# A scaled and re-split input for the first feed-forward product, in 512- and 256-column matmuls

## The chip, the cores and the metric

The kernel runs on one core of a Trainium2 chip. The metric is the device time of one execution in microseconds (us). The engines are PE (matrix multiply, with PEld for its weight loads), DVE (vector), ACT (scalar, activations), POOL (GpSimd) and SP (which issues DMAs).

## What is computed

A decoder trunk of two layers over 256 tokens and 1024 features: layer 0 with differential attention, layer 1 with latent attention, and in both a feed-forward block with a causal convolution and a gated per-layer embedding. The change touches the feed-forward block alone:

```python
def rms_norm(x, gain):
    y = xf * lax.rsqrt(jnp.mean(xf * xf, axis=-1, keepdims=True) + RMS_EPS)
    return (y * gain.astype(jnp.float32)).astype(x.dtype)

def conv_gated_ffn(h, w_in, conv_w, conv_b, w_out):     # w_in: 1024 x 5632, w_out: 2816 x 1024
    u = h @ w_in
    u_pad = jnp.pad(u, ((0, 0), (CONV_WIDTH - 1, 0), (0, 0)))
    c = conv_b
    for j in range(CONV_WIDTH):                          # 3 taps
        c = c + u_pad[:, j:j + s, :] * conv_w[j]
    a, g = jnp.split(c, 2, axis=-1)
    return (jax.nn.silu(g) * a) @ w_out

h = h + conv_gated_ffn(rms_norm(h, ffn_norm[i]), ...)    # once a layer
```

## The kernel before

All activations lie with features on the 128 partitions and the 256 tokens along the free dimension; `hT[:, k]` is the k-th of 8 blocks of 128 features of the residual stream. Products are kept near float32 by splitting each operand into a high part (rounded to fp32r by a cast on ACT) and a low part, the remainder (a subtraction). Weights come from one array, `wall`, in units of 128 x 1024 floats that are loaded in the order of use (`fetch`, on SP's queue), cast on ACT into `wh` and subtracted on DVE or POOL into `wl` (`split_unit`). `share[0]` says which: it is added up unit by unit, and each time the sum passes 1 that unit's subtraction goes to POOL.

`mm3` makes one contraction step of three matmuls of 256 columns (high x high, high x low, low x high), with two different weights, `wh` and `wl`. `mm2` makes the same step of two: `wh` against high and low part of the input side by side (512 columns, the results in the two halves of a bank), and `wl` against the high part (256 columns). The two halves have to be added afterwards. The second feed-forward product (`wst` with `wide`) already uses `mm2`.

`ffn` works through 22 pairs, i = 0 to 21: a pair is 128 columns of the value half and the same 128 of the gate half, two weight units, each with 8 contraction steps. The input `hgH`, `hgL` is the residual times the norm's gain, split, without the factor 1/rms of each token: that factor is not known when the product starts. `rstd_diag` and `rstd_rows` compute it during pairs 0 to 2 and leave it as `rb`, a tile with 1/rms of the tokens along the columns, the same on all partitions. `evac(i, ps)` multiplies the finished pair in PSUM by `rb` (L800, one instruction for both halves, since both lie in one bank), then makes the convolution (ACT L805, DVE L806 and L807), silu (ACT L809), the product (DVE L810) and the split for the second product (`g[i]`). Pairs that end before `rb` is there wait in `todo`.

The order on the engines is made by a scheduler that works from its own estimates when the program is built, so instructions of neighbouring pairs mix. Each engine then runs its list strictly in order. PSUM has 8 banks, which all pairs go round (`bankW`).

Of the kernel before, what the change touches and what calls it, by code (L numbers as in the profile page):

```python
# [14 lines left out]
ALU = mybir.AluOpType  # L15
# [4 lines left out]
P = 128  # L20
S = 256
NT = 2
D = 1024
NK = D // P
# [15 lines left out]
C_FFN = (32, 40)  # L40
# [38 lines left out]
RATIO_B = 1.7  # L79
BANKS_B = "ABACBACAACAA"  # L80
SH_A = 0.5
SH_FFN = 0.4
SH_PLE = 0.5
SH_B = 0.3

# [9 lines left out]
def trunk(ctx, tc, xT, xN, pT, pos, consts, grow, wall, out):  # L95
    nc = tc.nc
    V, A, G, T = nc.vector, nc.scalar, nc.gpsimd, nc.tensor
# [9 lines left out]
    def bank(tag):  # L107
        return pools[tag].tile([P, 512], F32, tag=tag, name="p" + tag.lower())
# [7 lines left out]
    def bankT():  # L116
        return bank("T")
# [6 lines left out]
    def bankW():  # L124
        nwide[0] += 1
        return bank("ACACA"[nwide[0] % 5])

    def d_tile(n=512, dt=F32):
        if dt == F32R:
            return tmp.tile([P, 512], F32R, tag="dr", name="dr", bufs=BUF_DR)[:, :n]  # L130
        return tmp.tile([P, 512], F32, tag="d", name="d", bufs=BUF_D)[:, :n]
# [10 lines left out]
    def f(ap):  # L142
        return ap.bitcast(F32)
# [11 lines left out]
    def run(gen):  # L155
        for c in gen:
            assert c is not None or late
            pump(c is None)
# [37 lines left out]
    def mm3(ps, aH, aL, bH, bL, start, stop):  # L196
        clk[0] += 3 * max(0.107, bH.shape[-1] * 0.000427)
        T.matmul(ps, lhsT=aH, rhs=bH, start=start, stop=False)  # L198
        T.matmul(ps, lhsT=aH, rhs=bL, start=False, stop=False)  # L199
        lastmm[0] = T.matmul(ps, lhsT=aL, rhs=bH, start=False, stop=stop).ins  # L200

    def mm2(ps, aH, aL, b, start, stop):


        n = b.shape[-1]
        clk[0] += 3 * max(0.107, n * 0.000427)
        T.matmul(ps[:, :2 * n], lhsT=aH, rhs=b.rearrange("p c n -> p (c n)"), start=start, stop=False)  # L207
        lastmm[0] = T.matmul(ps[:, :n], lhsT=aL, rhs=b[:, 0], start=False, stop=stop).ins  # L208

    def split(hi, lo, src, scale=None):  # L210
        if scale is None:
            return A.copy(hi, src).ins, V.tensor_sub(lo, src, f(hi)).ins  # L212
        return (A.activation(hi, src, AF.Copy, scale=scale).ins,
                V.scalar_tensor_tensor(lo, src, scale, f(hi), ALU.mult, ALU.subtract).ins)  # L214


    hT = cp.tile([P, NK, S], F32, name="hT")
# [10 lines left out]
    def fetch(pieces=1):  # L228
        st = ring.tile([P, UNIT], F32, tag="st", name="st", bufs=BUF_ST)
        u, n = unit_no[0], UNIT // pieces  # L230
        unit_no[0] += 1
        for j in range(pieces):
            lastfetch[0] = nc.sync.dma_start(st[:, j * n:(j + 1) * n], wall[u, :, j * n:(j + 1) * n]).ins
            if u in hooks:
                hooks.pop(u)()
            if pieces > 1:
                yield st
        if pieces == 1:
            yield st
# [4 lines left out]
    def split_unit(st, pair=None):  # L244
        hi, lo = pair or ring_pair()
        turn[0] += share[0]
        eng = V
        if turn[0] >= 1.0:
            turn[0] -= 1.0
            eng = G  # L250
        A.copy(hi, st)  # L251
        eng.tensor_sub(lo, st, f(hi))  # L252
        return hi, lo

    def load_unit():
        return split_unit(next(fetch()))
# [11 lines left out]
    def col(c, n=1):  # L268
        return cst[:, c:c + n]
# [21 lines left out]
    def og():  # L291
        return act.tile([P, 4, S], F32R, tag="og", name="og", bufs=8)

    def qk():
        return act.tile([P, 2, S], F32R, tag="qk", name="qk", bufs=BUF_QK)
# [33 lines left out]
    def rstd_rows(dg):  # L329
        with tc.high_priority(), tc.issue_after(lastmm[0]):  # L330
            ps = bankT()
            T.matmul(ps[:, :S], lhsT=ones, rhs=dg, start=True, stop=True)
            rb = act.tile([P, S], F32, tag="rb", name="rb", bufs=1)
            A.copy(rb, ps[:, :S])
        return rb
# [311 lines left out]
    def wst(order, b, post, bank=bankA, wide=0):  # L647

        kn = 1 + max(k for _, k in order)
        pss = {}  # L650
        for i, (n, k) in enumerate(order):
            z = i % 8
            if z == 0:
                u = load_unit()
            if k == 0:
                pss[n] = bank()
            ps, c, p = pss[n], slice(z * P, (z + 1) * P), b(k)
            if n < wide:
                mm2(ps, u[0][:, c], u[1][:, c], p, k == 0, k == kn - 1)
            else:  # L660
                mm3(ps[:, :S], u[0][:, c], u[1][:, c], p[:, 0], p[:, 1], k == 0, k == kn - 1)
            if k == kn - 1:
                add_h(n, ps[:, :S], post, ps[:, S:] if n < wide else None)
                del pss[n]
            if z == 7:
                yield 1
# [60 lines left out]
    def pre_load(l):  # L727

        share[0], was = 1.0, share[0]
        w = {"p": ple_p(l), "w": [split_unit(next(fetch()), ring_pair("x", 2)) for _ in range(2)]}  # L730
        share[0] = was
        return w
# [42 lines left out]
    def two(hgH, hgL, sq):  # L775

        ps = [bankW()[:, :S] for _ in range(2)]
        us = [load_unit() for _ in range(2)]
        for k in range(NK):
            for p, u in zip(ps, us):  # L780
                mm3(p, u[0][:, k * P:(k + 1) * P], u[1][:, k * P:(k + 1) * P], hgH[:, k], hgL[:, k], k == 0,
                    k == NK - 1)
            if k == NK - 3:
                dg = rstd_diag(sq)
        return ps, dg

    def ffn(l, st, post, mid=None):
        hgH, hgL = st["hg"]
        g = {}
        rb = None  # L790
        todo = []

        def evac(i, ps):
            if isinstance(ps, list):
                us = ps
                for u in us:
                    V.tensor_mul(u, u, rb)
            else:
                w = ps.rearrange("p (s t) -> p s t", s=2)
                V.tensor_mul(w, w, rb.unsqueeze(1).to_broadcast([P, 2, S]))  # L800
                us = w[:, 0], w[:, 1]
            cc = d_tile().rearrange("p (s t) -> p s t", s=2)
            for s in range(2):
                c0 = C_CONV[l] + 4 * (s * NF + i)
                A.activation(cc[:, s], us[s], AF.Identity, bias=col(c0 + 3), scale=col(c0 + 2))  # L805
                V.scalar_tensor_tensor(cc[:, s, 1:], us[s][:, :S - 1], col(c0 + 1), cc[:, s, 1:], ALU.mult, ALU.add)  # L806
                V.scalar_tensor_tensor(cc[:, s, 2:], us[s][:, :S - 2], col(c0), cc[:, s, 2:], ALU.mult, ALU.add)  # L807
            pr = us[0]
            A.activation(us[1], cc[:, 1], AF.Silu)  # L809
            V.tensor_mul(pr, us[1], cc[:, 0])  # L810
            if i >= 16:
                g[i] = qk()
            elif i % 2 == 0:
                gt = og()
                g[i], g[i + 1] = gt[:, 0:2], gt[:, 2:4]
            split(g[i][:, 0], g[i][:, 1], pr)

        for i in range(NF):
            if i == 0:
                share[0] = 0.0  # L820
                ps, dg = two(hgH, hgL, st["sq"])
            else:
                ps = bankW()
                for s in range(2):
                    wH, wL = load_unit()
                    for k in range(NK):
                        mm3(ps[:, s * S:(s + 1) * S], wH[:, k * P:(k + 1) * P], wL[:, k * P:(k + 1) * P], hgH[:, k],
                            hgL[:, k], k == 0, k == NK - 1)
                    if i == 1 and s == 0:
                        rb = rstd_rows(dg)  # L830
            if i == 2:
                share[0] = SH_FFN
            todo.append((i, ps))
            if i == 8 and mid:
                mid()
            while rb is not None and todo:
                evac(*todo.pop(0))
        if l == 0:
            pj.append(pre_load(1))
        share[0] = 0.0  # L840
        run(wst(FFN_OUT_ORDER, lambda k: g[k], post, bankW, NK - 1))
# [106 lines left out]
    actx.close()  # L948
    share[0] = SH_FFN
    pq = {}  # L950
# [3 lines left out]

    st2 = {}
    ffn(0, st, prep_post(C_PLE[0], st2), mid0)

    kvs = {}
# [282 lines left out]
    bctx.close()  # L1241
    share[0] = SH_FFN
    st2 = {}
    ffn(1, st, prep_post(C_PLE[1], st2))

    def out_post(n):
# [138 lines left out]
```

## Time and profile before

| | us |
|---|---|
| median of 3 runs | 770.49 (769.53 to 770.62) |
| the execution that was profiled | 770.32 |
| its span | 768.5 |
| PE busy in the span | 748.9 |
| DVE busy | 578.1 |
| ACT busy | 484.1 |
| POOL busy | 252.4 |

Busy times are of one profiled execution. Matmuls are pipelined: one of 256 columns is listed with 0.28 us though the next starts 0.12 us after it. So the rate of PE, and of DVE and ACT too, is read from start to start. In the timelines an idle stretch in front of an instruction stands in brackets with what ended it. The first product of layer 0 runs from about 155 to 278 us, that of layer 1 from about 550 to 675.

### The profile page before, as it was taken

How to read it: one execution, taken by the hardware profiler on the slowest of the kernel's cores; microseconds unless marked ns; L12 is line 12 of the kernel's file. 1: busy time of each engine (PE TensorE's matmuls, PEld its weight loads, DVE VectorE, ACT ScalarE, POOL GpSimd, SP SyncE). 2: the span in 40 equal slices, each digit the busy share in tenths (PEclk: the TensorE clock that was granted, in tenths of full speed). 3: DMA queues.
4: the chain of work that ended last, by engine and by line, in shares of the span. 5: the costliest groups of instructions: out<-in, count | busy, mean ns of one | idle time of the engine just before them, and what ended most of it. 6: DMA issues, size and time to landing. Idle time of an engine off the chain costs nothing.

```text
span 768.5 us, 15843 instructions
## 1 busy us (share of the span) xinstructions
PE 748.9 (97%) x6088; PEld 720.2 (94%) x6088; DVE 578.1 (75%) x1160; ACT 484.1 (63%) x1043; POOL 252.4 (33%) x176
## 2 busy tenths in 40 slices
PE   8999999999999999999999999999999999999996
PEld 6998988999999998899889998999999999988896
DVE  6667898568997787647688998877588778876545
ACT  6537777676666665547867776654676666655442
POOL 2654454233333420211214563421342332201230
PEclk9999999999999999999999999999999999999999
DMA  8994444255665576655355133334456555555531
GB/s 297 261 225 186 120 153 153 85 170 182 195 190 184 161 271 194 202 179 165 122 177 169 57 104 100 120 118 139 137 195 192 171 185 194 189 186 178 188 108 56
DMA packets 37517, 127.94 MB, mean 166 GB/s; under 512 B 4672, under 2 KB 6208, under 8 KB 37440
## 3 DMA queue, kind: packets, MB, share of 16 engines
q1 hardware_dynamic: 36432, 126.29, 51.9%
q8 instruction: 48, 0.79, 0.4%
q10 hardware_dynamic: 1008, 0.63, 0.3%
q14 instruction: 29, 0.24, 0.1%
HBM read 125.75 MB, written 1.15 MB: 165 GB/s over the span
## 4 chain that ended last, share of the span: by engine, by line
PE 80%; DVE 6%; ACT 6%; DMA 4%; POOL 2%; issue 2%; SPq 0%; ACTq 0%; DVEq 0%; POOLq 0%
PE pa L198 14%; PE pa L200 13%; PE pa L199 13%; PE pc L200 6%; PE pc L199 6%; PE pc L198 6%; PE pa L207 6%; PE pc L207 3%; PE pa L208 3%; DMA oh<-s 3%; PE pc L208 2%; ACT wh L251 2%; DVE wl L252 2%; POOL wl L252 1%; DMA st<-in_wall 1%
## 5 line engine op out<-in xcount | busy, mean ns | idle before, releaser
L251 ACT CAST wh<-st 128x1024 fp32r<-128x1024 f32 x221 | 230.8, 1049 | 153.0 <-issue 57.4
L252 DVE TENSOR_TENSOR wl<-st,wh 128x1024 fp32r<-128x1024 f32 x166 | 210.5, 1270 | 89.7 <-ACT wh L251 77.1
L252 POOL TENSOR_TENSOR wl<-st,wh 128x1024 fp32r<-128x1024 f32 x55 | 134.8, 2450 | 206.4 <-ACT wh L251 198.0
L200 PE MATMUL pa<-hgH,wl 128*128 128x256 f32 x496 | 141.2, 285 | 0.4 <-POOL wl L252 0.4
L199 PE MATMUL pa<-hgL,wh 128*128 128x256 f32 x496 | 140.3, 283 | 0.0
L198 PE MATMUL pa<-hgH,wh 128*128 128x256 f32 x496 | 140.1, 283 | 0.0
L309 POOL TENSOR_TENSOR ssq<-ssq,d 128x256 f32<-128x256 f32 x35 | 36.3, 1037 | 188.9 <-ACT d L308 174.1
L200 PE MATMUL pc<-hgH,wl 128*128 128x256 f32 x336 | 95.4, 284 | 0.9 <-DVE wl L252 0.9
L200 PEld LDWEIGHTS pa<-hgH,wl 128*128 128x128 f32 x496 | 95.2, 192 | 0.7 <-POOL wl L252 0.6
L198 PE MATMUL pc<-hgH,wh 128*128 128x256 f32 x336 | 95.1, 284 | 0.4 <-DVE pa L810 0.4
L198 PEld LDWEIGHTS pa<-hgH,wh 128*128 128x128 f32 x496 | 95.1, 192 | 0.1
L199 PEld LDWEIGHTS pa<-hgL,wh 128*128 128x128 f32 x496 | 95.2, 192 | 0.0
L199 PE MATMUL pc<-hgL,wh 128*128 128x256 f32 x336 | 95.1, 283 | 0.1
L198 PE MATMUL pa<-wh,hgH 128*128 128x256 f32 x320 | 92.0, 291 | 1.5 <-ACT wh L685 0.8
L199 PE MATMUL pa<-wl,hgH 128*128 128x256 f32 x320 | 91.8, 288 | 1.5 <-DVE wl L252 0.8
L200 PE MATMUL pa<-wh,hgL 128*128 128x256 f32 x320 | 91.2, 286 | 0.7 <-DVE hgL L212 0.7
L200 PEld LDWEIGHTS pc<-hgH,wl 128*128 128x128 f32 x336 | 64.5, 192 | 1.4 <-DVE wl L252 1.4
L198 PEld LDWEIGHTS pc<-hgH,wh 128*128 128x128 f32 x336 | 64.4, 192 | 0.8 <-DVE pa L810 0.6
L199 PEld LDWEIGHTS pc<-hgL,wh 128*128 128x128 f32 x336 | 64.4, 192 | 0.3 <-DVE hgL L214 0.3
L199 PEld LDWEIGHTS pa<-wl,hgH 128*128 128x128 f32 x320 | 61.6, 192 | 3.0 <-DVE wl L252 1.2
L198 PEld LDWEIGHTS pa<-wh,hgH 128*128 128x128 f32 x320 | 61.1, 193 | 3.0 <-ACT wh L685 1.1
L200 PEld LDWEIGHTS pa<-wh,hgL 128*128 128x128 f32 x320 | 61.6, 192 | 1.1 <-DVE hgL L212 0.9
(319 smaller groups left out, 1888.7 us busy)
## 6 DMA issues: line engine op xcount, KB each, us to landing
st<-in_wall SPq DMA_DIRECT2D x225, 512.0 KB, 3.7
oh<-s SPq DMA_DIRECT2D x24, 128.0 KB, 7.4
hT<-in_x SPq DMA_DIRECT2D x4, 256.0 KB, 5.1
st<-in_wall SPq DMA_DIRECT2D x4, 256.0 KB, 5.3
st<-in_xn SPq DMA_DIRECT2D x2, 512.0 KB, 7.0
d<-in_p SPq DMA_DIRECT2D x2, 256.0 KB, 4.7
out_h<-hT SPq DMA_DIRECT2D x4, 128.0 KB, 2.0
out_h<-hT ACTq DMA_DIRECT2D x4, 128.0 KB, 2.0
```

The costliest lines, as they stand in the source:

```text
L198: T.matmul(ps, lhsT=aH, rhs=bH, start=start, stop=False)
L199: T.matmul(ps, lhsT=aH, rhs=bL, start=False, stop=False)
L200: lastmm[0] = T.matmul(ps, lhsT=aL, rhs=bH, start=False, stop=stop).ins
L207: T.matmul(ps[:, :2 * n], lhsT=aH, rhs=b.rearrange("p c n -> p (c n)"), start=start, stop=False)
L208: lastmm[0] = T.matmul(ps[:, :n], lhsT=aL, rhs=b[:, 0], start=False, stop=stop).ins
L251: A.copy(hi, st)
L252: eng.tensor_sub(lo, st, f(hi))
L309: sqlast[0] = G.tensor_add(sq, sq, t).ins
```

## The change

For i = 4 on (`SCALED`), the factor `rb` moves from the result to the input. `scaled` makes, once a layer, eight pairs of tiles: `hT[:, k]` times gain times `rb` (DVE, one instruction), then the split (ACT cast, DVE subtraction), with high and low part side by side in one `qk` tile. The pairs from the fifth on use `mm2` on these tiles, and gate and value have a bank each. Their `evac` has no multiplication by `rb`; it copies the right half of each bank to SBUF (ACT) and adds it to the left half (DVE). The share of POOL is set one pair later and is 0.5 in place of 0.4.

```diff
-SH_FFN = 0.4
+SH_FFN = 0.5
+SCALED = 4
...
+    def scaled(g, rb):
+        hs = []
+        for k in range(NK):
+            x, pair = d_tile(S), qk()
+            V.scalar_tensor_tensor(x, hT[:, k], col(g + k), rb, ALU.mult, ALU.mult)
+            split(pair[:, 0], pair[:, 1], x)
+            hs.append(pair)
+        return hs
...
         def evac(i, ps):
-            if isinstance(ps, list):
+            if i >= SCALED:
+                lo = d_tile().rearrange("p (s t) -> p s t", s=2)
+                us = [p[:, :S] for p in ps]
+                for s in range(2):
+                    A.copy(lo[:, s], ps[s][:, S:])
+                    V.tensor_add(us[s], us[s], lo[:, s])
+            elif isinstance(ps, list):
...
-            else:
+            elif i < SCALED:
                 ps = bankW()
...
+            else:
+                ps = [bankW() for _ in range(2)]
+                for s in range(2):
+                    wH, wL = load_unit()
+                    for k in range(NK):
+                        mm2(ps[s], wH[:, k * P:(k + 1) * P], wL[:, k * P:(k + 1) * P], hs[k], k == 0, k == NK - 1)
             if i == 2:
+                hs = scaled(C_FFN[l], rb)
+            elif i == 3:
                 share[0] = SH_FFN
```

DVE in layer 0, from the first use of `rb`, before. `pc_2456` and `pa_2457` are the two banks of the first pair, `pc_2528` that of the second, `pa_2619` of the third; `d_` tiles hold the convolution, `og_` the input of the second product, `wl_` a weight remainder:

```order
L797 TENSOR_TENSOR pc_2456<-pc_2456,rb_2561 128x256
L797 TENSOR_TENSOR pa_2457<-pa_2457,rb_2561 128x256
L800 TENSOR_TENSOR pc_2528<-pc_2528,rb_2561 128x512
L800 TENSOR_TENSOR pa_2619<-pa_2619,rb_2561 128x512
L806 SCALAR_TENSOR_TENSOR d_2595<-pc_2456,cst_83,d_2595 128x255
L806 SCALAR_TENSOR_TENSOR d_2595<-pa_2457,cst_83,d_2595 128x255
L807 SCALAR_TENSOR_TENSOR d_2595<-pc_2456,cst_83,d_2595 128x254
L252 TENSOR_TENSOR wl_2800<-st_2797,wh_2799 128x1024
L807 SCALAR_TENSOR_TENSOR d_2595<-pa_2457,cst_83,d_2595 128x254
```

The same place now. L793 writes the scaled input (`d_2680` to `d_2700` are its first five pieces, the five rows in a row), and L213 on `qk_` is the subtraction that finishes a piece:

```order
L814 TENSOR_TENSOR pc_2456<-pc_2456,rb_2561 128x256
L814 TENSOR_TENSOR pa_2457<-pa_2457,rb_2561 128x256
L817 TENSOR_TENSOR pc_2528<-pc_2528,rb_2561 128x512
L817 TENSOR_TENSOR pa_2619<-pa_2619,rb_2561 128x512
L823 SCALAR_TENSOR_TENSOR d_2595<-pc_2456,cst_83,d_2595 128x255
L793 SCALAR_TENSOR_TENSOR d_2680<-hT_82,cst_83,rb_2561 128x256
```

DVE some 22 instructions later, up to the row that finishes the last of the eight pieces (`qk_2716`), and the two behind it; `og_2604<-pc_2456` is the last to read the first bank of the first pair:

```order
L817 TENSOR_TENSOR pa_2733<-pa_2733,rb_2561 128x512
L793 SCALAR_TENSOR_TENSOR d_2710<-hT_82,cst_83,rb_2561 128x256
L827 TENSOR_TENSOR pc_2456<-pa_2457,d_2595 128x256
L823 SCALAR_TENSOR_TENSOR d_2721<-pa_2619,cst_83,d_2721 128x255
L213 TENSOR_TENSOR qk_2706<-d_2705,qk_2706 128x256
L823 SCALAR_TENSOR_TENSOR d_2795<-pa_2733,cst_83,d_2795 128x255
L213 TENSOR_TENSOR qk_2711<-d_2710,qk_2711 128x256
L213 TENSOR_TENSOR qk_2716<-d_2715,qk_2716 128x256
L824 SCALAR_TENSOR_TENSOR d_2721<-pa_2619,cst_83,d_2721 128x254
L213 TENSOR_TENSOR og_2604<-pc_2456,og_2604 128x256
```

Between the first use of `rb` and the row of `qk_2716` there stand now 32 instructions, both counted; before, the first evacuations went on at once.

PE where the fourth pair (`pa_2693`) ends and the next begins, before:

```order
L198 MATMUL pa_2693<-hgH_2343,wh_2726 128x256
L199 MATMUL pa_2693<-hgL_2344,wh_2726 128x256
L200 MATMUL pa_2693<-hgH_2343,wl_2727 128x256
L198 MATMUL pa_2840<-hgH_2343,wh_2843 128x256
L199 MATMUL pa_2840<-hgL_2344,wh_2843 128x256
```

And now; `pa_2733` is the fourth pair, `pa_2807` the gate's bank of the fifth:

```order
L199 MATMUL pa_2733<-hgH_2343,wh_2766 128x256
L200 MATMUL pa_2733<-hgL_2344,wh_2766 128x256
L201 MATMUL pa_2733<-hgH_2343,wl_2767 128x256
L208 MATMUL pa_2807<-qk_2681,wh_2832 128x512
L209 MATMUL pa_2807<-qk_2681,wl_2833 128x256
```

The fifth pair now reads the scaled tiles (`qk_`) from its first matmul on. Its other bank, `pc_2806`, comes after it and is the one that `pc_2456` had. On POOL, one weight remainder a pair now stands in the list from the fifth pair on; on ACT, eight casts of `qk_` tiles stand among the casts of `wh_`, in front of the table load for silu. SP's order is the same as before.

## Rows read from the trace of the kernel before

**Rows 1.** The page, part 4: shares of the chain that ended last

```profile
PE 80%; DVE 6%; ACT 6%; DMA 4%; POOL 2%; issue 2%; SPq 0%; ACTq 0%; DVEq 0%; POOLq 0%
```

**Rows 2.** By stretch: length; busy PE, PEld, DVE, ACT, POOL; clock, DMA share, GB/s

```profile
160.00:280.00 120.00, 119.62 (x990) 119.13 (x990) 102.73 (x200) 80.17 (x133) 42.83 (x18) 1.00 0.62 196
```

**Rows 3.** Timeline of PE (start, length, line, operands, [idle]): first, second product

```profile
202.10 0.28 PE L198 MATMUL pa<-hgH,wh 128*128 128x256 f32 x1
...
260.06 0.28 PE L198 MATMUL pa<-hgH,wh 128*128 128x256 f32 x1
...
301.61 0.40 PE L207 MATMUL pa<-og,wh 128*128 128x512 f32 x1
...
306.47 0.40 PE L207 MATMUL pa<-og,wh 128*128 128x512 f32 x1
...
692.07 0.40 PE L207 MATMUL pa<-og,wh 128*128 128x512 f32 x1
...
720.34 0.40 PE L207 MATMUL pa<-qk,wh 128*128 128x512 f32 x1
```

**Rows 4.** Timeline of PE where the fifth pair begins, layer 0 and layer 1

```profile
173.86 0.28 PE L199 MATMUL pa<-hgL,wh 128*128 128x256 f32 x1
174.52 0.39 PE L200 MATMUL pa<-hgH,wl 128*128 128x256 f32 x1 [0.38 <-POOL wl L252]
...
571.06 0.28 PE L200 MATMUL pc<-hgH,wl 128*128 128x256 f32 x1
571.70 0.39 PE L198 MATMUL pc<-hgH,wh 128*128 128x256 f32 x1 [0.35 <-DVE pa L810]
```

**Rows 5.** Timeline of DVE from the first use of rb, layer 0 and layer 1

```profile
167.04 0.43 DVE L797 TENSOR_TENSOR pc<-pc,rb 128x256 f32<-128x256 f32 x1 [2.80 <-ACT rb L334]
167.38 0.42 DVE L797 TENSOR_TENSOR pa<-pa,rb 128x256 f32<-128x256 f32 x1
...
168.31 0.69 DVE L800 TENSOR_TENSOR pa<-pa,rb 128x512 f32<-128x512 f32 x1
168.91 0.47 DVE L806 SCALAR_TENSOR_TENSOR d<-pc,cst,d 128x255 f32<-128x255 f32 x1
169.30 0.47 DVE L806 SCALAR_TENSOR_TENSOR d<-pa,cst,d 128x255 f32<-128x255 f32 x1
...
170.08 1.22 DVE L252 TENSOR_TENSOR wl<-st,wh 128x1024 fp32r<-128x1024 f32 x1
171.21 0.48 DVE L807 SCALAR_TENSOR_TENSOR d<-pa,cst,d 128x254 f32<-128x254 f32 x1
...
564.43 0.43 DVE L797 TENSOR_TENSOR pa<-pa,rb 128x256 f32<-128x256 f32 x1
```

**Rows 6.** Timelines of POOL (first row) and DVE around 210 us

```profile
210.14 2.40 POOL L252 TENSOR_TENSOR wl<-st,wh 128x1024 fp32r<-128x1024 f32 x1 [6.17 <-ACT wh L251]
...
210.62 1.97 DVE L928 TENSOR_TENSOR rak<-cst,d 128x32 f32<-128x32 f32 x1
212.51 0.18 DVE L929 TENSOR_TENSOR rak<-cst,d 128x32 f32<-128x32 f32 x1
212.62 0.18 DVE L928 TENSOR_TENSOR rak<-cst,d 128x32 f32<-128x32 f32 x1
```

**Rows 7.** Timelines of ACT and POOL behind the third pair, layer 1

```profile
565.55 1.05 ACT L251 CAST wh<-st 128x1024 fp32r<-128x1024 f32 x1
...
566.67 2.41 POOL L252 TENSOR_TENSOR wl<-st,wh 128x1024 fp32r<-128x1024 f32 x1 [4.67 <-ACT wh L251]
```

**Rows 8.** By stretch (columns as in rows 2), and timeline of PE inside it

```profile
420.00:440.00 20.00, 19.86 (x156) 19.14 (x156) 17.22 (x50) 16.28 (x55) 12.34 (x14) 0.91 0.25 80
...
419.59 0.30 PE L198 MATMUL pb<-qk 128*128 128x128 f32 x1 [1.21 <-DVE s L358]
...
424.40 0.41 PE L198 MATMUL pa<-wh,hgH 128*128 128x256 f32 x1
424.61 0.41 PE L199 MATMUL pa<-wl,hgH 128*128 128x256 f32 x1
```

## The prediction

> **What bounds the kernel now.** I read the chain of waits on the page first: 80% of the span is PE, VectorE (DVE) and ScalarE (ACT) hold 6% each [rows 1]. The table by stretch then shows the first feed-forward product of layer 0: in 120 us PE is busy for 119.62, at a granted clock of 1.00, while DVE is busy for 102.73, ACT for 80.17 and GpSimd (POOL) for 42.83 [rows 2]. So a matmul saved in this product is time saved, as long as nothing makes PE wait; and DVE, at 86%, is the engine with least room to take more. Last I read the timelines of PE, DVE, ACT and POOL where the fifth pair (i = 4) begins.
>
> **The matmuls.** 18 pairs of 16 contraction steps in two layers are 576 steps. Before, a step is three 256-column matmuls: from 202.10 to 260.06 us there are 161 steps, 57.96/161 = 0.360 us each. The second product already uses the new form, one of 512 columns and one of 256: from 692.07 to 720.34 us there are 80 steps, 28.27/80 = 0.353 us; the best stretch, 301.61 to 306.47, has 14 steps of 0.347 us [rows 3]. The same 768 columns are streamed, so the gain is small: 576 x 0.0066 = 3.8 us, at best 576 x 0.0129 = 7.4. I take 3.8, since the even stretch is longer. The Trainium skill (TensorE: Matmul & The Clock Gate, Back-to-back issue gap) gives columns/2.4 + 2.5 ns a matmul; by that a step saves only one 2.5 ns term, my estimate is 1.4 us, and the end would be 2.4 us later than below. The rows show more, and the measurement decides.
>
> **The evacuation.** Per pair one 512-element multiply by rb goes from DVE (0.60 us from start to start) and two 256-element additions come (0.34 each), so +0.08; the larger POOL share (one of the pair's two weight remainders in place of 0.8) takes 0.2 x 1.13 from DVE [rows 5]. ACT gets two copies of 256 more. All of this lies beside 16 x 0.353 = 5.65 us of PE per pair: DVE needs 2 x 0.34 + 4 x 0.39 + 0.34 + 0.34 + 1.13 = 4.05 us. I cost it at nothing. If a 2.40 us POOL remainder [rows 6] were to hold DVE up in every pair, 6.45 us would exceed 5.65, and 0.8 us a pair would show.
>
> **The scaled input, the term that decides.** rb exists only late in the third pair. DVE stands there with the evacuation of the first pairs queued behind it: its first use of rb is at 167.04 us, and PE begins the fifth pair at 173.74, one matmul before the row at 173.86 [rows 4, 5]. The fifth pair now needs all eight scaled pieces: 8 multiplications and 8 subtractions on DVE, 8 casts on ACT. In the new order the last of those subtractions is the 32nd DVE instruction after rb. Those 32 are 3 sums or products of 256 (0.34), 3 of 512 (0.60), 9 STT (scalar_tensor_tensor) of the convolution (0.39), 8 STT of the scaling (as the convolution's, 0.39), 8 subtractions (0.34, as the products of 256) and one weight remainder (1.13): 1.0 + 1.8 + 3.5 + 3.1 + 2.7 + 1.1 = 13.2 us [rows 5]. So the last piece is ready at about 167.04 + 13.2 + 0.1 = 180.35, and PE wants it at 173.74 + 7 x 0.353 = 176.2. Two instructions later the bank of the second half comes free, at 181.1, where PE without a wait would be at 173.74 + 2.83 = 176.57: **4.5 us of stall**. ACT does not hide or shorten it: it is queued in front of silu with a weight cast that waits for the end of the fourth pair, but DVE is still behind at that point. In layer 1 the first use of rb is at 564.43 and the fifth pair starts at 571.18 (0.12 after 571.06, without the pause): 6.75 us against 6.70, so 4.5 again. What waits behind: PE runs in order, nothing else stands in it, and PE never gets a stall back.
>
> Two pauses of before go: 173.86 to 174.52 is 0.66 where 0.12 is normal, 571.06 to 571.70 is 0.64 [rows 4]. They are **1.06 us** together; both waits (a POOL remainder, a bank) are now met earlier or lie inside the stall.
>
> **The port between DVE and POOL.** In the trace of before a DVE instruction with both inputs in SBUF stands still while POOL subtracts a weight remainder: the 32-element product that starts at 210.62 takes 1.97 us, its followers are 0.1 apart, and the next one starts at 212.51, when the POOL instruction of 210.14 (2.40 us) ends at 212.54 [rows 6]. The evacuation reads PSUM, so before little was exposed. The 16 new instructions read hT, rb, d and qk: all SBUF. POOL's first remainder of the fifth pair follows the ACT cast behind the third pair: in layer 1 POOL starts at 566.67 [rows 7], and DVE reaches its first scaling at 564.43 + 0.34 + 0.34 + 0.60 + 0.60 + 0.39 = 566.70. In layer 1 the cast (565.55) starts 0.13 after the fourth pair (571.18 - 48 x 0.12 = 565.42) and POOL 1.12 after the cast; in layer 0 that gives 173.74 - 5.76 + 0.13 + 1.12 = 169.23, against 167.04 + 2.27 = 169.31 for DVE. So POOL is there first, and DVE waits 2.3 us. POOL's next remainder follows the cast that waits for the end of the fourth pair (173.74 + 0.13 + 1.12 = 175.0 at the earliest); DVE is then at its own remainder and the subtractions behind it, and I count 2.0 of the 2.40 us. Bounds: 0, when DVE is first both times, to 4.8. I take **4.3 us a layer**, the sum of the two.
>
> **The clock.** During some 9 us PE issues a few matmuls at a time. In 420:440, after an idle of 1.21 us in front of 419.59, the granted clock has a mean of 0.91, and two matmuls stand 0.21 apart (424.40, 424.61) where 0.12 is normal: the lower level, 1.2 GHz [rows 8]. That cost 0.09 x 20 = **1.8 us** of work at 2.4 GHz. I take one such fall a layer; bounds 0 and two falls.
>
> **Sum.** 2 x (4.5 + 4.3 + 1.8) = 21.2; less 1.06 and 3.8: +16.3 us on the execution that was profiled, 770.32 us. That is 0.17 us below the median of the runs shown, so it stands for it: **786.6 us**. With the bounds of the lock and the clock this case covers 780 to 793.
>
> **Rivals.** First, the lock costs nothing: the two instructions in question lie 0.03 to 0.08 us apart in my sums, and if DVE comes first POOL is the one that waits, and its remainders have pairs of slack. Then 9.0 + 0 to 3.6 - 4.9 = +4.1 to +7.7, **776 us**. For it: the narrow margin; against it: the second meeting is between a stream of short DVE instructions and a waiting POOL. The Trainium skill (SBUF — State Buffer, Who interferes with whom) says that whichever starts first has the port pair for its whole instruction and the other blocks; by that this rival needs no more than DVE's early start, and the rows of before, where POOL started first, agree with the rule.
>
> Second, faster: the scaled input is hidden, since DVE runs its 32 instructions quicker than the spacings of the rows. Place: between rb and the ninth half-pair. It decides from 13.2 down to about 8.7 us for the 32, 0.27 us each; then only the gains are left, 770.32 - 4.9 = **765 us**, or 762 at the best step. Against it: the spacings are DVE's own rate, not waits.
>
> Third, no change: no lock, no fall of the clock, and every step of the new form at the best stretch's 0.347: 9.0 - 1.06 - 7.4 = +0.5, **770.8 us**. It asks for three things together.
>
> Fourth, worse: the lock also binds in the steady pairs, as bounded above, 0.8 us in a third of 34 pairs and more: +9, **796 us** and up. For it: POOL now has a remainder in every pair. Against it: remainders of POOL and DVE follow casts that are half a pair, 2.8 us, apart, more than 2.40.
>
> **How the numbers follow.** Forecast 0.62, first rival 0.20, faster 0.04, no change 0.04, worse 0.10. The range 775 to 794 takes in the forecast's bounds and the first rival. About 0.2% is what a measurement of this kernel can tell from no change. Faster 0.04, same 0.04, slower 0.92.
>
> **What would show it.** In the profile after: 512-column matmuls of the first product 0.353 us a step apart in steady pairs; PE waiting at the fifth pair for the subtraction of the scaled pieces, about 9 us in each layer over some ten matmuls; scaling or subtraction instructions of DVE of 1 to 2.5 us that end with a POOL remainder; a window with a clock below 1.00 near 180 and near 578; no waits of PE in later pairs. I am wrong if the fifth pair starts without a wait, if the stall is near 4.5 us with DVE instructions of normal length (first rival), or if PE waits for wl in many pairs (fourth).

## The result

The changed kernel takes 791.01 us (789.6 to 792.41, median of 4 runs), the kernel before 770.56 in the same comparison: a ratio of 1.0272 with a 95% interval of 1.0257 to 1.0287. The forecast was 786.6, range 775 to 794. The execution that was profiled took 790.56 us, of which the span is 788.8.

The page of the changed kernel, busy times and the chain that ended last (the chain answers to [rows 1]):

```profile
span 788.8 us, 14846 instructions
PE 750.9 (95%) x5512; PEld 693.7 (88%) x5512; DVE 591.1 (75%) x1222; ACT 510.3 (65%) x1131; POOL 271.4 (34%) x182
...
PE 77%; DVE 12%; ACT 6%; issue 2%; DMA 1%; POOL 1%; SPq 0%; ACTq 0%; POOLq 0%; DVEq 0%
```

PE is busy for about as long as before (750.9 against 748.9); the span is 20.3 us longer, and 18.3 of that is idle time of PE (37.9 against 19.6). So PE hardly does more, it waits, and DVE's share of the chain has doubled from 6 to 12%. The table by stretch shows where (columns as in [rows 2], first the stretch of [rows 2] itself):

```profile
160.00:280.00 120.00, 109.95 (x642) 96.31 (x640) 99.21 (x212) 84.12 (x159) 47.50 (x20) 0.96 0.54 171
180.00:200.00 20.00, 17.69 (x88) 14.94 (x87) 18.33 (x43) 14.44 (x31) 4.83 (x2) 0.80 0.38 127
580.00:600.00 20.00, 11.69 (x55) 9.98 (x54) 18.80 (x42) 13.50 (x29) 5.35 (x2) 0.74 0.28 95
```

In the 120 us in which PE had been idle for 0.4 it is now idle for 10, and at the fifth pair of either layer, where PE waits, DVE is busy for 18.3 and 18.8 of 20 us and the granted clock of those stretches is 0.80 and 0.74.

What PE waits for in the two first products, by tile and releaser (us in total, times, longest; the first three rows are 165 to 300 us, the last two 570 to 700):

```profile
PE pa L208 <- DVE qk L213: 6.2, 4, 2.3
PE pa L209 <- POOL wl L253: 3.1, 2, 2.1
PE pa L208 <- DVE pc L827: 1.5, 1, 1.5
...
PE pc L208 <- DVE pa L827: 8.3, 1, 8.3
PE pa L208 <- DVE pc L827: 2.9, 2, 1.5
```

The 6.2 and the 8.3 us are the fifth pairs. In layer 0 PE waits four times for a scaled piece (`qk` L213 is the subtraction that finishes one). In layer 1 it waits once: there the half-pair that comes first takes the bank that the first pair had, and L827, the product of value and gate, is the last to read that bank. The other 7.5 us come in later pairs.

The same places in PE's timeline, from the last matmul of the old form to the first step at full pace:

```profile
173.32 0.28 PE L201 MATMUL pa<-hgH,wl 128*128 128x256 f32 x1
174.76 0.50 PE L208 MATMUL pa<-qk,wh 128*128 128x512 f32 x1 [1.16 <-DVE qk L213]
...
188.19 0.39 PE L208 MATMUL pc<-qk,wh 128*128 128x512 f32 x1
...
580.10 0.28 PE L201 MATMUL pa<-hgH,wl 128*128 128x256 f32 x1
588.68 0.79 PE L208 MATMUL pc<-qk,wh 128*128 128x512 f32 x1 [8.31 <-DVE pa L827]
...
594.38 0.40 PE L208 MATMUL pa<-qk,wh 128*128 128x512 f32 x1
```

Layer 0: from 173.44, where the new form could have begun, to 188.19 are 14.75 us with 13 steps, which take 4.51 at full pace: 10.2 lost. Layer 1: from 580.22 to 594.38 are 14.16 us with 9 steps (3.16): 11.0 lost. Of these 21.2 us 14.5 are the waits above, and 6.7 are steps at the lower level of the clock and the restarts: after 588.68 steps stand 0.64 apart where 0.35 is normal.

And the DVE and POOL rows behind it, layer 0 (start, length; x5 and x2 are neighbours taken together):

```profile
166.74 0.43 DVE L814 TENSOR_TENSOR pc<-pc,rb 128x256 f32<-128x256 f32 x1
...
169.00 4.21 DVE L793 SCALAR_TENSOR_TENSOR d<-hT,cst,rb 128x256 f32<-128x256 f32 x5
...
176.83 2.52 DVE L213 TENSOR_TENSOR qk<-d,qk 128x256 fp32r<-128x256 f32 x2
...
183.29 0.75 DVE L213 TENSOR_TENSOR qk<-d,qk 128x256 fp32r<-128x256 f32 x2
...
168.93 2.41 POOL L253 TENSOR_TENSOR wl<-st,wh 128x1024 fp32r<-128x1024 f32 x1 [5.93 <-ACT wh L252]
175.35 3.38 POOL L253 TENSOR_TENSOR wl<-st,wh 128x1024 fp32r<-128x1024 f32 x1 [4.01 <-ACT wh L252]
```

From the first use of `rb` to the last piece are 17.3 us (166.74 to 184.04); the forecast had 13.2 + 4.3. Five multiplications take 4.21 us, though 0.39 each would be 1.95: POOL's remainder ended at 171.34. Two subtractions take 2.52, though 0.7 would do; POOL's second remainder ends at 178.73, and it too is long, 3.38 where 2.41 is normal.

### The profile page after: what moved, and what is told of

It is laid out like the page before. It is cut to its first block, busy times and chain, and to the rows that moved or that the text cites. A ratio compares the mean times of both kernels' runs of the same rounds, so it can differ in the third digit from the quotient of the medians.

```text
span 788.8 us, 14846 instructions
## 1 busy us (share of the span) xinstructions
PE 750.9 (95%) x5512; PEld 693.7 (88%) x5512; DVE 591.1 (75%) x1222; ACT 510.3 (65%) x1131; POOL 271.4 (34%) x182
## 4 chain that ended last, share of the span: by engine, by line
PE 77%; DVE 12%; ACT 6%; issue 2%; DMA 1%; POOL 1%; SPq 0%; ACTq 0%; POOLq 0%; DVEq 0%
PE pa L208 12%; PE pc L208 10%; PE pa L199 9%; PE pa L200 9%; PE pa L201 9%; PE pa L209 6%; PE pc L209 5%; DVE wl L253 4%; PE pc L201 3%; PE pc L200 3%; PE pc L199 3%; ACT wh L252 2%; PE pt L193 1%; DVE d L793 1%; PE pc L193 1%
## 5 line engine op out<-in xcount | busy, mean ns | idle before, releaser
L208 PE MATMUL pa<-qk,wh 128*128 128x512 f32 x392 | 141.2, 400 | 10.6 <-DVE qk L213 6.2
L209 PE MATMUL pa<-qk,wl 128*128 128x256 f32 x392 | 110.7, 282 | 3.1 <-POOL wl L253 3.1
L208 PE MATMUL pc<-qk,wh 128*128 128x512 f32 x268 | 98.6, 406 | 8.3 <-DVE pa L827 8.3
L208 PEld LDWEIGHTS pa<-qk,wh 128*128 128x128 f32 x392 | 74.3, 190 | 29.8 <-DVE qk L213 7.8
L209 PEld LDWEIGHTS pa<-qk,wl 128*128 128x128 f32 x392 | 74.8, 191 | 3.9 <-POOL wl L253 3.7
L209 PE MATMUL pc<-qk,wl 128*128 128x256 f32 x268 | 76.8, 286 | 0.0
L208 PEld LDWEIGHTS pc<-qk,wh 128*128 128x128 f32 x268 | 52.1, 194 | 20.5 <-DVE pa L827 8.5
L200 PE MATMUL pa<-og,wh 128*128 128x256 f32 x208 | 59.0, 285 | 0.9 <-DVE og L215 0.9
L199 PE MATMUL pa<-og,wh 128*128 128x256 f32 x208 | 59.2, 290 | 0.1
L201 PE MATMUL pa<-og,wl 128*128 128x256 f32 x208 | 59.2, 286 | 0.0
L209 PEld LDWEIGHTS pc<-qk,wl 128*128 128x128 f32 x268 | 52.3, 195 | 0.5 <-DVE wl L253 0.3
```

## Experiments

All times are medians beside runs of the kernel before on the same chip, the ratios to it with their 95% intervals. "Changed" is the changed kernel, 791.0 us.

### Is it the port? e1 and e2

**e1**: the scaling reads 1/rms from the PSUM tile in which it is computed.

```diff
             A.copy(rb, ps[:, :S])
+        rbps[0] = ps[:, :S]
         return rb
...
-            V.scalar_tensor_tensor(x, hT[:, k], col(g + k), rb, ALU.mult, ALU.mult)
+            V.scalar_tensor_tensor(x, hT[:, k], col(g + k), rbps[0], ALU.mult, ALU.mult)
```

> The eight scaling multiplications read 1/rms from the PSUM bank in which it is computed, not from its SBUF copy, so they have one SBUF input in place of two; order and everything else as changed. Theory (DVE and POOL share a port for SBUF): the group of five multiplications takes 5 x 0.39 = 1.95 us, not 4.21 and 4.26 as in the changed kernel, DVE is 2.3 us earlier in each layer, and the time is 791.0 - 4.5 = 786.5 us (785 to 788). The two subtractions that took 2.5 us still do, since they read SBUF twice, if a POOL remainder is then running. Rival (the multiplications are long for a reason of their own, and POOL's remainder beside them is chance): the group of five stays above 4 us and the time at 791.

Measured: 784.43 us, ratio 1.019 (1.016 to 1.0221): 6.6 us less than the changed kernel. DVE, then POOL, then PE:

```profile
169.35 2.04 DVE L796 SCALAR_TENSOR_TENSOR d<-hT,cst,pt 128x256 f32<-128x256 f32 x5
...
175.01 0.75 DVE L213 TENSOR_TENSOR qk<-d,qk 128x256 fp32r<-128x256 f32 x2
...
175.00 2.97 POOL L253 TENSOR_TENSOR wl<-st,wh 128x1024 fp32r<-128x1024 f32 x1 [3.29 <-ACT wh L252]
...
178.07 0.77 PE L208 MATMUL pa<-qk,wh 128*128 128x512 f32 x1 [4.12 <-DVE d L796]
...
581.82 0.79 PE L208 MATMUL pc<-qk,wh 128*128 128x512 f32 x1 [4.32 <-DVE pa L830]
```

The same five multiplications, beside a POOL remainder as before (169.28 to 171.70), take 2.04 us when one input comes from PSUM. So the stall was for the second SBUF input. The two subtractions still read SBUF twice, but now they and POOL's remainder begin at the same time, and POOL pays (2.97 in place of 2.41), not DVE: 1.8 us a layer that the expectation had left in, and of which layer 0 does not get the whole. DVE's 32 instructions now take 13.3 us (167.09 to 180.43), the 13.2 of the forecast without the port. What is left at the fifth pairs is one wait in either layer: in layer 0 for the bank in which 1/rms itself lies, released by the last multiplication, a cost of this experiment; in layer 1 for the bank of the first pair again. The waits in later pairs are still 7.5 us. The Trainium skill (SBUF — State Buffer, Who interferes with whom) says that a DVE instruction with two SBUF inputs contends with a GpSimd instruction that reads SBUF and one with a single SBUF input outside certain modes does not, and that issue order decides who blocks. The traces agree on the inputs, with 4.21 against 2.04 us. On the order they agree where it can be read: in the changed kernel POOL's second remainder began first (175.35 against 176.83) and DVE stood still; in layer 1 of e1 DVE's two subtractions began at 578.50 and POOL's remainder at 578.59, and POOL's was the long one (2.88). In layer 0 of e1 the starts lie 0.01 us apart, too near to tell.

**e2**: POOL's share begins two pairs later.

```diff
-            elif i == 3:
+            elif i == 5:
                 share[0] = SH_FFN
```

> POOL's share of the weight remainders begins two pairs later, so POOL has no remainder while DVE makes the scaled input; DVE gets two remainders more (1.13 us each) ahead of the last scaled piece, 35 instructions in place of 32. Theory (port): the five multiplications take 1.95 us and the two subtractions 0.7, DVE gains 2.3 + 1.85 and loses 2.3 us in each layer: 1.8 us a layer, 787 us (785.5 to 789). Rival (no port, only DVE's own instructions): the two remainders lengthen the stall by 2.3 us a layer, 795.6 us.

Measured: 788.82 us, ratio 1.0242 (1.022 to 1.0264), 2.2 us less where 3.6 was expected, at the upper end of the range; the rival would have lengthened it to 795.6. Without a POOL instruction from 163 to 188 us the five multiplications take 2.06 us with both inputs in SBUF:

```profile
168.54 2.06 DVE L793 SCALAR_TENSOR_TENSOR d<-hT,cst,rb 128x256 f32<-128x256 f32 x5
...
188.70 2.42 POOL L253 TENSOR_TENSOR wl<-st,wh 128x1024 fp32r<-128x1024 f32 x1 [26.16 <-DVE og L213]
```

So it is POOL's company that makes them long. But DVE then makes the two remainders itself, and the last piece is ready 16.0 us after the first use of `rb` (166.28 to 182.31) in place of 17.3.

### Who waits for what? e3 and e4

**e3**: the scaled input is made, and nothing reads it; all pairs are as before the change.

```diff
-            if i >= SCALED:
+            if i >= NF:
...
-            elif i < SCALED:
+            elif i < NF:
                 ps = bankW()
```

> The scaled input is made as in the changed kernel, but nothing reads it: all pairs use the three 256-column matmuls on the unscaled input, one bank a pair, as before the change. The share of POOL is that of the changed kernel. Theory A (as the prediction put it: PE waits because the fifth pair needs the eight pieces): no piece is needed, the stall of the fifth pair goes, 771 to 773 us. Theory B (the 16 instructions on DVE delay the evacuation of the first pairs, and PE waits for the bank of the first pair or a remainder that is queued behind them, whoever needs the pieces): PE still waits 6 to 9 us in each layer, in layer 1 at the fifth pair for the bank of the first, 783 to 788 us.

Measured: 782.2 us, ratio 1.0154 (1.0132 to 1.0176). Theory A falls. Theory B has the mechanism, but its 783 to 788 us were a little too much. PE's waits in the two first products (the first two rows are layer 0):

```profile
PE pa L201 <- DVE wl L253: 2.3, 1, 2.3
PE pc L201 <- POOL wl L253: 1.0, 1, 1.0
...
PE pc L199 <- DVE pa L827: 6.4, 1, 6.4
```

Nobody needs a scaled piece here, and still 11.9 us are lost: at the fifth pair of layer 0 PE waits 2.3 us for a weight remainder that stands in DVE's list behind the scaling, less than the 6 to 9 of theory B, and in layer 1 at the fifth pair for the bank of the first pair, 6.4 us. So the pieces are not the only thing that is late. Sixteen instructions put ahead of the waiting evacuations make everything late that DVE does behind them, and in layer 1 PSUM has no spare bank to bridge that.

**e4**: the kernel before with the new share alone.

```diff
-SH_FFN = 0.4
+SH_FFN = 0.5
...
-            if i == 2:
+            if i == 3:
                 share[0] = SH_FFN
```

> The kernel before with the new share alone: 0.5 in place of 0.4, set one pair later. The prediction costed it at nothing: 770.5 us, within 0.2%. Rival (the share makes POOL's remainders late, as the two waits for POOL in the changed kernel, 1.04 and 2.07 us, suggest): PE waits for POOL in some pairs of the first product, 772 to 774 us.

Measured: 771.76 us, ratio 1.0026 (1.001 to 1.0043), runs from 770.3 to 775.4. PE waits for POOL nowhere in the first product, and the two feed-forward stages (from the sum for the norm ahead of the block to that behind it) take 185.6 and 188.0 us, against 186.2 and 188.0 before. So the share costs nothing where it acts; the extra of the profiled execution (775.0) lies in the attention between, 214.6 us against 209.8, where its clock was 0.83 in one stretch of 20 us. The waits for POOL that the rival took from the changed kernel are not from the share by itself.

### Where do the later waits come from? e5 and e6

**e5**: the 512-column form without the scaled input; 1/rms is left out of these pairs.

```diff
-        return (act.tile([P, NK, S], F32R, tag="hgH", name="hgH"),
-                act.tile([P, NK, S], F32R, tag="hgL", name="hgL"))
+        t = act.tile([P, 2 * NK, S], F32R, tag="hgH", name="hgH")
+        hg2[0] = t.rearrange("p (k c) s -> p k c s", c=2)
+        return (hg2[0][:, :, 0], hg2[0][:, :, 1]) if side else (t[:, :NK], t[:, NK:])
...
-                        mm2(..., hs[k], k == 0, k == NK - 1)
-            if i == 2:
-                hs = scaled(C_FFN[l], rb)
-            elif i == 3:
+                        mm2(..., st["hg2"][:, k], k == 0, k == NK - 1)
+            if i == 3:
```

> The two-bank form without the scaled input: from the fifth pair on the 512- and 256-column matmuls run on the unscaled input, kept side by side, and nothing is made on DVE ahead of them. The factor 1/rms is left out of these pairs altogether, so the output isn't the reference's; the copy, the addition and the rest of the evacuation are as in the changed kernel, and POOL's share too. Theory (bank: two banks a pair make PE wait for the evacuation later on, whatever the fifth pair does): no stall at the fifth pair, and waits for a bank or for POOL of 5 to 12 us in both layers together, as the 8.3 us of the changed kernel; the shorter steps give back 6.2, so 770 to 777 us. Rival (the later waits of the changed kernel are after-effects of its stall): the later waits go too, 764 to 766 us.

Measured: 781.78 us, ratio 1.0158 (1.0144 to 1.0173): above both. There is no stall of a microsecond at the fifth pair, and yet PE waits for 9 us in layer 0 and 4.8 in layer 1, in later pairs, mostly for banks and DVE's remainders. The two longest, in PE's timeline:

```profile
216.71 0.50 PE L208 MATMUL pa<-hgH,wh 128*128 128x512 f32 x1 [3.21 <-DVE og L213]
...
249.58 0.50 PE L208 MATMUL pa<-hgH,wh 128*128 128x512 f32 x1 [2.18 <-DVE pc L831]
```

So the later waits are no after-effect of the stall; the form brings them. The size was missed: without the stall they are longer, not equal. Chain alone +11.9, form alone +11.9, both +20.4: two losses, of which some 3 us overlap.

**e6**: the product goes to SBUF, so that the value's bank is free some instructions earlier.

```diff
-            pr = us[0]
+            pr = us[0] if i < SCALED else cc[:, 0]
             A.activation(us[1], cc[:, 1], AF.Silu)
             V.tensor_mul(pr, us[1], cc[:, 0])
```

> As the changed kernel, but from the fifth pair on the product of value and gate is written to the SBUF tile of the convolution and not over the value in PSUM, so the value's bank comes free after the second tap of the convolution, some 2 to 3 us earlier. Theory (bank): the three later waits for a bank (1.55, 1.34, 1.55 us) go, the stall at the fifth pair stays: 791.0 - 4.4 = 786.6 us (784.5 to 788). Rival (port: the split of the product now reads SBUF twice and stands still beside POOL's remainders): DVE loses up to 2 us in some pairs and the later waits stay or grow, 791 to 797.

Measured: 780.63 us, ratio 1.0146 (1.013 to 1.0162), 10.4 us less than the changed kernel where 4.4 was expected. PE's waits (the last row is layer 1):

```profile
PE pa L208 <- DVE qk L213: 6.2, 4, 2.3
PE pc L208 <- DVE d L827: 1.4, 1, 1.4
...
PE pc L208 <- DVE pa L827: 6.4, 1, 6.4
```

The three waits for a bank are gone as expected, one of 1.4 us is new; the two for POOL went with them, and layer 1's stall is 6.4 in place of 8.3. The bank waits, 4.4 us less the new 1.4, can be put down to the bank that is held for two DVE instructions less: the banks bind. The rest came with another order from the scheduler: in layer 1 DVE now makes five scaling multiplications from 570.30 in 2.06 us, before POOL's remainder begins at 572.12. Why the new order also frees POOL's remainders was not taken apart. The port cost of the split that now reads SBUF twice did not show in PE's waits.

### All three causes met: e9, e10, e7, e8

**e9** is e1 and e6 together.

> Two of the three edits of the kernel that beat the one before: the multiplications read 1/rms from PSUM, and the product goes to SBUF; the scaled input stays where the change has it (made after the third pair, used from the fifth). Theory (the two cures act at different places, so their gains of 6.6 and 10.4 us add up, and what is left is DVE's own backlog, a stall of 4 us in each layer at the fifth pair): 791.0 - 17.0 = 774 us (772 to 777). Rival (they overlap, since both shorten the same stall): 777 to 780.

Measured: 775.47 us, ratio 1.008 (1.0064 to 1.0096). This is the theory: of the two gains, 17.0 together, 15.5 are there, and what is left is 4.1 and 4.2 us of wait at the fifth pairs and 1.4 later.

**e10** moves the scaled input alone.

```diff
-SCALED = 4
+SCALED = 9
...
-            if i == 2:
+            if i == 5:
                 hs = scaled(C_FFN[l], rb)
-            elif i == 3:
+            if i == 3:
                 share[0] = SH_FFN
```

> The third edit alone: the scaled input is made after the sixth pair and used from the tenth on; 1/rms from SBUF, product in PSUM, as in the changed kernel. Theory (the stall at the fifth pair is one loss, the later waits another, and this edit takes away the first alone): 770.6 less 4.5 for the steps, plus 5 to 8 us of later waits, 771 to 775. Rival (a wait moves with the form: where two banks a pair and the 16 instructions meet, PE waits for a bank again, 4 us or more at the tenth or eleventh pair): 776 to 782.

Measured: 782.35 us, ratio 1.0163 (1.0146 to 1.018): the rival, 0.35 us above its range. In layer 1 the feed-forward stage takes 188.4 us, nearly what it took before (188.0), but in layer 0 the waits have moved along with the form, to the eleventh and twelfth pairs:

```profile
216.28 0.80 PE L208 MATMUL pa<-qk,wh 128*128 128x512 f32 x1 [3.85 <-DVE og L213]
...
223.64 0.80 PE L208 MATMUL pa<-qk,wh 128*128 128x512 f32 x1 [2.91 <-DVE pc L827]
```

DVE has the tables for layer 1's rotation to make there as well, which would explain the difference between the layers; no run separates it.

**e7** has all three edits (those of e1, e6 and e10), **e8** the same with the form from the thirteenth pair, made after the seventh, and a share of 0.45.

> Three edits on the changed kernel: the scaled input is made after the sixth pair and used from the tenth on, when DVE has no first pairs waiting; its multiplications read 1/rms from PSUM; the product of value and gate goes to SBUF from the tenth pair on. 13 pairs a layer keep the new form: 208 steps x (0.0132 in layer 0 and 0.0085 in layer 1, as measured in the changed kernel) = 4.5 us less than before the change. Theory (the loss is DVE's backlog behind 1/rms, the port and the banks, and all three are met): no wait over 1 us in the first product, 766 to 769 us, just under the kernel before. Rival (the change to two banks a pair brings a wait of its own wherever it begins): a wait of 4 us or more at the tenth pair or the one behind it, 772 us and up.

> As the run before it, but the scaled input is made after the seventh pair and used from the thirteenth, and POOL's share is 0.45. 10 pairs a layer keep the new form: 160 steps x (0.0132 + 0.0085) = 3.5 us less than before the change. Theory: waits of some 1 to 3 us in the first product, 768 to 770.5 us. Rival: as there, 772 us and up.

Measured: e7 766.17 us, ratio 0.9951 (0.9938 to 0.9965); e8 766.71, ratio 0.9959 (0.9944 to 0.9974). Both beat the kernel before and the changed one, e7 within the range of its theory, e8 below its own (768 to 770.5). In e7 PE waits in layer 0 for 3.2 us and in layer 1 for nothing of 0.2 us or more; the main row of layer 0:

```profile
PE pc L209 <- POOL wl L253: 2.7, 2, 1.6
```

Both waits for POOL are above the microsecond that the theory allowed (1.6 and 1.1). From the changed kernel the edits are worth 6.6, 10.4 and 8.7 us each by itself and 24.8 together.

**e11 and e12**: the kernel before and e7, each a second time, without an edit. The reason: of the 3.5 us between the two profiled executions only 0.7 lay in the two feed-forward stages.

> The kernel before, unchanged, for a second trace. In the kernel that beat it, 3.2 of the 3.5 us between the two profiled executions lay in the attention of layer 1, between the two feed-forward blocks (from the norm's sum behind the first to that behind the second: 206.58 us against 209.79), a stage that no edit touches. Theory (chance: where the clock falls in that stage differs from execution to execution): this trace has another length there, 206.5 to 208.5 or above 211. Rival (the order that the scheduler gives there differs for good): 209.8 again, within 0.4, with the fall of the clock at 420 to 440.

> The same for the kernel that beat the one before (run e7), unchanged. Theory (chance): the stage between has a length that differs from 206.58 by more than 0.5 us. Rival (for good): 206.6 within 0.4 again. Either way the time is 766.2 within 1.5 us, and the two feed-forward stages 187.6 and 185.9 within 0.5.

Measured: 769.61 us (ratio 0.9999, 0.9989 to 1.0009) and 765.63 (0.9945, 0.993 to 0.996). The norm sums that divide the stages, in e11:

```profile
161.05 0.50 PE L314 MATMUL pt<-ones,ssq 128*128 128x2 f32 x4
347.25 0.50 PE L314 MATMUL pt<-ones,ssq 128*128 128x2 f32 x4
...
557.10 0.50 PE L314 MATMUL pt<-ones,ssq 128*128 128x2 f32 x4
745.08 0.50 PE L314 MATMUL pt<-ones,ssq 128*128 128x2 f32 x4
```

The stage between takes 209.85 us, as in the first trace (209.79), though this time no stretch of it has a clock below 1.00. So there the kernel before is steady, and the rival holds for it. e7 has 206.58 and 207.75 (the second with a clock of 0.91 in one stretch): it does vary, by more than 0.5 as the theory of chance has it, but is shorter both times. So most of the shorter length there belongs to the program, though no edit touches the stage. The other traces say the same: in the ten of kernels that make the scaled input the stage takes 206.6 to 208.5 us, in the four of kernels that do not (the one before twice, e4, e5) 209.8 to 214.6. That the scheduler's order of it differs is argued, and which instruction makes it was not searched. The feed-forward stages of e12, 187.1 and 185.9, make 1.2 us of the gain, against 186.2 and 188.0 before. So most of what e7 gains over the kernel before does not come from the product that was changed.

## Why the prediction was right, and where not

The norm sums of the changed kernel:

```profile
160.24 0.50 PE L315 MATMUL pt<-ones,ssq 128*128 128x2 f32 x4
358.19 0.50 PE L315 MATMUL pt<-ones,ssq 128*128 128x2 f32 x4
...
565.57 0.50 PE L315 MATMUL pt<-ones,ssq 128*128 128x2 f32 x4
764.84 0.50 PE L315 MATMUL pt<-ones,ssq 128*128 128x2 f32 x4
```

The feed-forward stages take 197.95 and 199.27 us, 11.7 and 11.3 more than in e11's trace and in that of before; the stage between takes 207.38, 2.5 less.

| term (us, both layers) | forecast | measured |
|---|---|---|
| fifth pairs: DVE, port, clock | 21.2 | 21.2 |
| shorter steps | -3.8 | -6.2 |
| pauses of before gone | -1.1 | -1.1 |
| waits in later pairs | 0 | 7.5 |
| stages outside | 0 | -2.7 |
| not accounted for | | 1.5 |
| sum | 16.3 | 20.2 |

**The deciding term came out at its size, in part by luck.** DVE's 32 instructions take 13.3 us without the port (e1) and 17.3 with it; the port held up both places that were named, by 2.3 and 1.8 us; both fifth pairs fell to a lower clock. But the clock and the restarts cost 6.7 us, not 3.6, and the waits 14.5, not 17.6; that these two misses cancel is luck. The waits are shorter since the pieces come one by one, so that in layer 0 PE does some steps between the waits. The price of a fall of the clock, 1.8 us, came from the stretch of [rows 8]. In e11 that stretch has no fall, and the stage around it is as long (209.85 against 209.79); e7 and e12, one program without and with such a fall, are 1.2 us apart there. So no run shows 1.8; the fifth pairs lost 4.0 and 2.7 us beside their waits.

**The prediction named the need for the eight pieces as the mechanism** and the bank only as the next thing late. The traces make the bank at least its equal. In layer 1 the changed kernel waits for the bank alone; in e3 and e6, where DVE's list there runs in the same order, PE waits 6.45 and 6.43 us, though only e6 reads the pieces. In layer 0 PE does wait for the pieces, 6.2 us against 2.3 at the fifth pair of e3. But the second half of the fifth pair takes the bank that the first pair had, and in the changed kernel this is the last instruction to read that bank, and the first to write it anew:

```profile
184.34 0.41 DVE L213 TENSOR_TENSOR og<-pc,og 128x256 fp32r<-128x256 f32 x1
...
185.20 0.63 PE L208 MATMUL pc<-qk,wh 128*128 128x512 f32 x1
```

The bank comes free at 184.75, 0.45 us before PE takes it. So without the need for the pieces the stall would have moved to the bank; that is worked out from these rows, no run has it.

**The first rival** (the lock costs nothing, 776) fell: POOL was first at 168.93, 0.07 before DVE's first multiplication, by the narrow margin that was worked out (0.08); in layer 1 the margin is 0.02 (0.03). At the second meeting the order is open by a hair: in layer 0 of e1 both begin within 0.01 us, and POOL loses.

**The wrong step is "lies beside other work"** for the evacuation. It was costed at nothing from DVE's busy time per pair (4.05 of 5.65 us). That sum holds in the main (from 595 to 650 us DVE is busy for 41.9 of 55, 76% where the sum has 72%), but it counts the work and not how long a bank is held: with two banks a pair the eight banks go round in four pairs, and the way from copy and addition over the convolution and silu to the product has become longer. PE waited five times, for 7.5 us, three times for a bank (4.4) and twice for POOL (3.1). The fourth rival had the sign and a price (9 us), but another mechanism, POOL in a third of the steady pairs; e6 took all five waits away with an edit that touches a bank and, through the scheduler, the order. What made the two for POOL is not shown.

**The gain of the steps was mis-sized**, 3.8 for 6.2. Rows of the form in steady pairs, layer 0 and layer 1:

```profile
222.09 0.40 PE L208 MATMUL pa<-qk,wh 128*128 128x512 f32 x1
...
256.77 0.39 PE L208 MATMUL pa<-qk,wh 128*128 128x512 f32 x1
...
595.07 0.40 PE L208 MATMUL pa<-qk,wh 128*128 128x512 f32 x1
...
652.73 0.40 PE L208 MATMUL pa<-qk,wh 128*128 128x512 f32 x1
```

100 steps in 34.68 us are 0.347 each, 164 in 57.66 are 0.352. Layer 0 runs at the best stretch of [rows 3], layer 1 between the two: 288 x 0.0132 + 288 x 0.0085 = 6.2. The Trainium skill's gap (TensorE: Matmul & The Clock Gate, Back-to-back issue gap) had led to an estimate of 1.4. It is given there for an isolated matmul, with the warning that a stream with weight loads is spaced otherwise. The measurement decides against the estimate here.

So the number came within 4.4 us because two misses of 7.5 and -5.1 us (steps and outside) partly cancel, and those within the deciding term wholly; the rest, 1.5, is not assigned. One sum of the prediction does not come out: the bounds that it gives for the lock (0 to 4.8 us a layer) and the clock (none to two falls) make 774 to 791 us, not 780 to 793, so the measured time lies at the upper end of them.

## What to carry to other kernels

A step that is moved from the result to the input saves work on paper but lands where a whole queue waits for the same late value; count what stands behind it in the engine's list, and test it as e3 does, by making the value and not using it. An engine's busy share says whether the work fits, not whether a buffer comes back in time: when a change doubles the banks of a stage, follow one bank from its last matmul to its last reader. And where a DVE instruction must read two operands beside a busy POOL, taking one of them from PSUM was worth 4.21 against 2.04 us for five instructions here.

## What was not expected of the hardware

The step of one 512- and one 256-column matmul has two lengths that repeat: 0.347 us in layer 0 and 0.351 to 0.352 in layer 1, in e1, e2, e6, e7 and e8 as in the changed kernel. In e5, which reads another tile, both occur in either layer: in layer 0, 40 steps from 199.11 have 0.347 and 87 from 250.04 have 0.353. No run tells why.

The port also holds up a DVE instruction with one tensor input. In the changed kernel a 64-element operation took 2.28 us beside POOL, where its like takes 0.19 elsewhere in the trace:

```profile
207.30 2.28 DVE L941 TENSOR_SCALAR d<-d 128x64 f32<-128x64 f32 x1
...
207.13 2.40 POOL L253 TENSOR_TENSOR wl<-st,wh 128x1024 fp32r<-128x1024 f32 x1 [3.17 <-ACT wh L252]
```

It ends at 209.58, 0.05 after POOL's. Layer 0 of e10 has two more, of 1.33 and 1.62 us, that end 0.05 and 0.06 after a remainder of POOL. So "two SBUF inputs" is not the whole condition.
